# The low parts of split weights: VectorE takes the subtractions that Pool took in turn

## The chip, the core and the metric

The kernel runs on one core of a Trainium2 chip. The metric is the device time of one execution in microseconds (us). The engines are TensorE (PE, matrix products; its weight loads are listed as PEld), VectorE (DVE), ScalarE (ACT), GpSimd (Pool) and SyncE (SP), whose queue issues most DMAs. Each engine works through its own instructions in order and waits for the others by semaphores.

## The reference

Two blocks of network follow each other on 256 tokens of width 1024, everything in float32:

```python
def first_block(x, ...):                       # two layers
    for l in range(DEPTH):
        mix = even_mixer(...) if l % 2 == 0 else odd_mixer(...)
        x = layer_norm(ALPHA * x + mix, ln_g[l, 0], ln_b[l, 0])
        ffn = routed_moe(x, router_w, router_b, moe_w_gate[l], moe_w_up[l], moe_w_down[l])
        x = layer_norm(ALPHA * x + ffn, ln_g[l, 1], ln_b[l, 1])

def second_block(x, c, ada_w, ada_b, ...):     # two layers of three sublayers
    mod = c_act @ ada_w[layer] + ada_b[layer]  # shift, scale, gate of each sublayer
    x = x + 0.5 * (1 + gate) * swiglu(modulate(x, 0), ...)
    x = x + (1 + gate) * (hybrid_mixer | mlstm_block)(modulate(x, 1), ...)
    x = x + 0.5 * (1 + gate) * swiglu(modulate(x, 2), ...)

def swiglu(h, w_gate, w_up, w_down):
    return (jax.nn.silu(h @ w_gate) * (h @ w_up)) @ w_down
```

What matters here is that every weight is used once, for 256 tokens, and that most products are wanted more exact than one pass of PE gives.

## The kernel before, in words

The program is ten phases, one after the other, named by letters: A the even attention mixer, B its experts, C the odd attention mixer, D its experts, and then in the second block E, G, H and J, the four SwiGLU feed-forward sublayers, with F (the hybrid of a linear recurrence and a state-space layer) between E and G, and I (the mLSTM) between H and J.

The weights of all phases come from memory in one long sequence of 1 MB DMAs (128 partitions of 2048 floats, `load_weights`, L507), issued from SP. Each holds two chunks of 128x1024. The chunks land in blocks of a common pool of 23 blocks of 8 KB per partition; a block is given back when the work on it is done, and the next DMA of the sequence waits for a free block. A dry run beforehand fixes at which points of the program DMAs are issued.

A chunk of the ordinary weights is split before use (`new_split`, L579): ACT copies it rounded to the 32-bit format that PE takes in one pass (the high part, L586), and a second engine subtracts that copy from the chunk to give the low part (L587). A product is then three passes on PE (L594): high by high, low by high, high by low. PE's passes on a chunk can begin with the high part, but not end without the low one. The two expert phases B and D use their weights unsplit, so L587 doesn't appear there.

Which engine subtracts is what the change is about. In the kernel before, `pool=True` sends a subtraction to Pool; besides, a counter `nsplit` sends every third one there, every fourth in C, G and H, every sixth in F (`POOL_SPLIT`). Two places pause that: after the gate weights of the mLSTM are prepared `no_pool` counts 14 splits, and after each recurrence of F six. All others go to DVE.

`pool=True` is given at two places: `following` (L967) makes the first splits of the next phase while the last one ends, and does so with Pool for phases C and E (three and three); `enter` (L891) makes one more at the start of E.

Other work on the same queues, which the numbers below name:
- L545, in `ada_step`: the modulation of the second block (`mod`) is a product of one vector with a very long weight matrix. Its chunks come in the same sequence of DMAs, and DVE multiplies each by the vector and adds up, in one instruction over 128x1024 floats. These stand between the splits, at points that the plan fixes.
- L646 and L647: the high part (ACT) and the low part (DVE) of an activation, 128x256.
- L1858 and L1999: convolution and state products of F on DVE, with small tiles.
- L2088 to L2103, `gate_weights`: in the middle of phase H, 864 KB of gate columns for phase I are loaded, Pool clears a buffer (L2091), and builds the gate weights by small multiplications and additions (L2099, L2102, L2103). The block that the columns lay in is free after the last of them.
- L800 to L815 and L853 to L897: the layer norm at the end of a layer of the first block and the norm behind it, one token block of 128 after the other.

The order within each engine is set by a scheduler that takes the program's order as base and lets some instructions go earlier by a priority (`sooner`, with `SPLIT_AHEAD` for splits and `ADA_AHEAD` for L545), according to the costs it assumes for each engine.

Of the kernel before, what the change touches and what calls it, by code (L numbers as in the profile page):

```python
# [322 lines left out]
class Pipe:  # L323


    def __init__(self, sooner):
        self.waiting, self.flying, self.sooner = [], [], sooner
# [40 lines left out]

SLACK = {'A': 5, 'B': 3, 'C': 7, 'D': 2, 'E': 6, 'F': 7, 'G': 7, 'H': 7, 'I': 6, 'J': 7}

POOL_SPLIT = {'C': 4, 'F': 6, 'G': 4, 'H': 4}
POOL_TURN = {}
POOL_P = ''

PIECES = ((slice(0, 512), slice(512, 1024)),) * 2
# [18 lines left out]
class Net:  # L394
    NBLK = 23

    def __init__(self, ctx, tc, aps, phases, plan=None, at=None):
        self.tc, self.nc, self.aps, self.phases = tc, tc.nc, aps, phases
        self.blk = ctx.enter_context(tc.tile_pool(name="blk", bufs=1))
        self.cst = ctx.enter_context(tc.tile_pool(name="cst", bufs=1))  # L400
        self.sm = ctx.enter_context(tc.tile_pool(name="sm", bufs=2))
        self.pp = ctx.enter_context(tc.tile_pool(name="pp", bufs=4, space=bass.MemoryType.PSUM))
        self.issue_at, self.at = plan, at or {}
        self.free = [(-64, 0, b) for b in range(self.NBLK if plan is not None else 64)]
        self.own, self.nfree = {}, 0
        self.uid = 0
        self.nchunk = sum(NCH[p] for p in phases)
        self.ndma = (self.nchunk + 1) // 2
        self.issued = 0
        self.ring = {}  # L410
        self.pos = 0
        self.nsplit, self.phase, self.last_mm, self.last_pe = 0, None, [], None
        self.held, self.no_pool = [], 0
        self.hold, self.closed, self.span = False, [], {}
        self.pre, self.guard, self.guarded, self.evac = [], [], 0, None
        self.first, self.last, self.left = {}, {}, {}
# [162 lines left out]
    def new_split(self, n, pool=False):  # L579
        i, w = self.raw()  # L580
        u, t = self.alloc([128, 2, 1024], F32R)
        self.nsplit += 1
        self.no_pool -= 1
        eng = self.nc.gpsimd if pool or self.no_pool < 0 and (self.nsplit + POOL_TURN.get(self.phase, 0)) % POOL_SPLIT.get(self.phase, 3) == 0 else self.nc.vector
        with self.sooner(SPLIT_AHEAD.get(self.phase, 0)):
            self.nc.scalar.activation(t[:, 0, :n], w[:, :n], AF.Copy)  # L586
            eng.tensor_tensor(t[:, 1, :n], w[:, :n], t[:, 0, :n].bitcast(F32), op=OP.subtract)  # L587
        self.taken(i)
        return u, t[:, 0, :n], t[:, 1, :n]
# [1218 lines left out]
    def phase_ffn(self, l, s, nxt):  # L1808
        nc = self.nc
        us, xt, room = self.entry  # L1810
        token = self.first4(xt, room)
        acc = self.acc4()
        nt = 6
        items, hl = [], []
        ur, ring = self.alloc([128, 4, 2, S], F32R)
        for f in range(24):
            if f == 22 - nt:
                uk = [self.alloc([128, 4, 2, S], F32R) for _ in range(nt // 3)]
            if f < 22:
                if f < 4:  # L1820
                    u = self.p1(xt, ps=self.ph)
                    g = token(f)
                else:
                    g = self.p1(xt, ps=self.ph)
                    u = self.p1(xt, ps=self.ph)
                a = self.w0()
                i = f - 22 + nt
                p = uk[i // 4][1][:, i % 4] if i >= 0 else ring[:, f % 4]
                nc.scalar.activation(a, g, AF.Silu)  # L1829
                nc.vector.tensor_tensor(a, a, u, op=OP.mult)  # L1830
                self.hilo(a, p[:, 0, :], p[:, 1, :])
                hl.append((p[:, 0, :], p[:, 1, :]))
                if f == 6 and nxt == (1, 1):
                    self.gate_weights()
                    self.no_pool = 14
                if f == 21:
                    self.warm(AF.Sqrt, a)
                    self.prep_gate(l, s)
                    if nxt:
                        self.prep(*nxt)  # L1840
            if f >= 24 - nt:
                items.append((hl[f - 2], self.split()))
            elif f >= 2:
                self.row(acc, hl[f - 2], f == 2, False)
            if f == 23 - nt:
                self.release(ur)
        self.release(*us)
        self.tail(acc, items, self.gated(l, s, self.following()))
        self.release(*(u for u, _ in uk))
# [11 lines left out]
    def phase_F(self):  # L1861
# [26 lines left out]
        def gates(h):  # L1888
            rec[h] = self.alloc([128, 2, 4, S])
            for j in range(4):  # L1890
                n = 4 * h + j
                for a, bname in enumerate(('lba', 'lbx')):
                    ps = self.ph()
                    self.mm(ps[:, :S], ws[a][:, n, :], xl[:, n, :])
                    nc.scalar.activation(rec[h][1][:, a, j, :], ps[:, :S], AF.Sigmoid, bias=self.col(bname, n))

        def recur(h):
            u, ri = rec[h]
            r, gi, tt = ri[:, 0], ri[:, 1], tts[:, h]
            for j in range(4):  # L1900
                n = 4 * h + j
                nc.scalar.activation(tt[:, j, :], r[:, j, :], AF.Tanh, scale=lam[:, 1, n:n + 1])
                nc.scalar.activation(r[:, j, :], r[:, j, :], AF.Exp, scale=lam[:, 0, n:n + 1])
                a2 = self.w0()
                nc.gpsimd.tensor_tensor(a2, r[:, j, :], r[:, j, :], op=OP.mult)
                v.scalar_tensor_tensor(tt[:, j, :], a2, 1.0, tt[:, j, :], op0=OP.add, op1=OP.mult)
                nc.gpsimd.tensor_tensor(gi[:, j, :], gi[:, j, :], xl[:, n, :], op=OP.mult)
            nc.scalar.activation(flat(tt), flat(tt), AF.Sqrt)
            for j in range(4):
                n = 4 * h + j  # L1910
                nc.gpsimd.tensor_tensor(tt[:, j, :], tt[:, j, :], gi[:, j, :], op=OP.mult)  # L1911
                v.tensor_tensor_scan(xl[:, n, :], r[:, j, :], tt[:, j, :], 0.0, op0=OP.mult, op1=OP.add)
            self.release(u, lag=1)

        for i in range(8):
            self.conv(token(i) if i < 4 else self.p1(xt), 'lcw', 'lcb', i, xl[:, i, :])
            if i == 3:
                wa = self.raw()
                self.ada_step()
                wx = self.raw()  # L1920
                self.ada_step()
                ws = [a[1].rearrange("p (n o) -> p n o", n=8) for a in (wa, wx)]
            if i == G0:
                gates(0)
            if i == R0:
                recur(0)
                self.no_pool = 6
        uz, zz = self.alloc([128, 8, S])
        for i in range(8):
            v.tensor_copy(zz[:, i, :], self.p1(xt))  # L1930
            if i == G1:
                gates(1)
                self.done(wa[0])
                self.done(wx[0])
            if i == R1:
                recur(1)
                self.no_pool = 6
        self.release(utt, lag=2)
        uhi, yhi = self.alloc([128, 8, S], F32R)
        ulo, ylo = self.alloc([128, 8, S], F32R)  # L1940
# [454 lines left out]
```

## Time and profile before

| | |
|---|---|
| median of 3 runs | 1922.91 us (1920.03 to 1923.42) |
| profiled execution | 1923.58 us, of which the span from first to last instruction 1921.9 |
| PE busy | 1842.1 us (96%) |
| DVE busy | 1196.6 us (62%) |
| ACT busy | 879.4 us (46%) |
| Pool busy | 460.7 us (24%) |
| mean granted clock of TensorE | 0.986 of full speed |
| subtractions L587 | 297 on DVE, 117 on Pool |

The busy times are sums over stages with different limits. In the rows further down, a timeline row gives the start (us from the begin of the span), the duration, the engine, the line and operation, the tile written and those read, and in brackets how long the engine had stood idle and what it had waited for. "t" is any block of the pool, "pg" and "ph" are PSUM tiles, "kc" a constant.

### The profile page before, as it was taken

The numbers are of one execution on the slowest core, as the hardware profiler recorded it, in microseconds if no ns is written. First come the engines' busy times: TensorE is split into PE (matmuls) and PEld (weight loads), VectorE is DVE, ScalarE is ACT, GpSimd is POOL, SyncE is SP. The second block draws the span as 40 slices with busy tenths as digits, with TensorE's granted clock in tenths as the row PEclk, the third lists the DMA queues.
The fourth block names the chain that finished last, engine by engine and source line by source line (L and its number), as shares of the span: only waits on it lengthen the run. The fifth ranks groups of instructions, "written<-read, shape, count | busy, mean of one in ns | idle before, by whom it ended". The sixth has DMA issues, their size and how long they took to land.

```text
span 1921.9 us, 29062 instructions
## 1 busy us (share of the span) xinstructions
PE 1842.1 (96%) x11556; PEld 1477.0 (77%) x11556; DVE 1196.6 (62%) x1948; ACT 879.4 (46%) x1523; POOL 460.7 (24%) x295
## 2 busy tenths in 40 slices
PE   7999999889999998999999999999999999999998
PEld 7874544577544547999898779998899888879997
DVE  5862221586422229899699987767797665576453
ACT  5641111355221125445686644455345566655443
POOL 2200000231000004334243222222423213443232
PEclk9999999989999998999999999999999999999999
DMA  9569999565899996883435478647674615555520
GB/s 386 225 239 389 422 420 421 235 234 209 332 420 421 420 421 269 349 339 150 163 132 219 165 295 324 268 178 295 254 322 176 258 72 181 212 208 211 198 88 34
DMA packets 70975, 507.01 MB, mean 264 GB/s; under 512 B 7856, under 2 KB 8112, under 8 KB 10032
## 3 DMA queue, kind: packets, MB, share of 16 engines
q1 hardware_dynamic: 70256, 503.15, 65.9%
q8 instruction: 92, 1.51, 0.3%
q10 hardware_dynamic: 576, 1.93, 0.3%
q14 instruction: 51, 0.42, 0.1%
HBM read 504.00 MB, written 1.05 MB: 263 GB/s over the span
## 4 chain that ended last, share of the span: by engine, by line
PE 45%; DVE 10%; POOL 4%; ACT 3%; issue 3%; DMA 2%; DVEq 0%; POOLq 0%; ACTq 0%
PE ph L594 27%; PE pg L594 16%; DVE t L587 3%; DMA t<-in_weights 2%; DVE t L1858 2%; PE ph L599 1%; DVE t L545 1%; POOL t L587 1%; ACT t L586 1%; POOL w L2266 1%; POOL t L1911 0%; POOL t L2103 0%; DVE t L1999 0%; ACT ph L851 0%; ACT t L1855 0%
## 5 line engine op out<-in xcount | busy, mean ns | idle before, releaser
L594 PE MATMUL pg<-t,t 128*128 128x512 f32 (+4 forms) x4702 | 941.1, 403 | 27.4 <-DVE t L587 9.9
L594 PEld LDWEIGHTS pg<-t,t 128*128 128x128 f32 (+1 forms) x4702 | 674.7, 180 | 236.8 <-issue 126.0
L594 PE MATMUL ph<-t,t 128*128 128x256 f32 (+3 forms) x4550 | 589.5, 290 | 7.5 <-ACT t L2130 2.3
L594 PEld LDWEIGHTS ph<-t,t 128*128 128x128 f32 (+2 forms) x4550 | 564.5, 192 | 23.5 <-issue 3.1
L586 ACT ACTIVATE t<-t 128x1024 fp32r<-128x1024 f32 (+4 forms) x414 | 425.0, 1049 | 255.9 <-DVE t L587 73.0
L587 POOL TENSOR_TENSOR t<-t,t 128x1024 fp32r<-128x1024 f32 (+2 forms) x117 | 303.8, 2601 | 882.7 <-ACT t L586 778.4
L587 DVE TENSOR_TENSOR t<-t,t 128x1024 fp32r<-128x1024 f32 (+1 forms) x297 | 414.8, 1412 | 107.1 <-ACT t L586 105.6
L545 DVE SCALAR_TENSOR_TENSOR t<-t,cact 128x1024 f32<-128x1024 f32 x144 | 222.7, 1558 | 34.6 <-DMA t<-in_weights 30.8
L594 PE MATMUL ph<-t,w 128*64 128x512 f32 (+3 forms) x696 | 161.5, 547 | 0.0
L594 PEld LDWEIGHTS ph<-t,w 128*64 128x64 f32 (+1 forms) x696 | 68.4, 145 | 73.7 <-issue 63.5
L1353 DVE TENSOR_TENSOR w<-w,pg 128x512 f32<-128x512 f32 x16 | 10.9, 684 | 154.7 <-ACT w L1352 154.7
L1352 ACT ACTIVATE w<-pg 128x512 f32<-128x512 f32 x16 | 9.6, 598 | 186.4 <-PE pg L594 186.4
L646 ACT ACTIVATE t<-w 128x256 fp32r<-128x256 f32 x107 | 43.8, 411 | 107.1 <-DVE w L1830 94.8
L1381 DVE SCALAR_TENSOR_TENSOR t<-ph,rgsl,t 128x512 fp32r<-128x512 f32 x32 | 24.0, 751 | 108.4 <-ACT t L1380 108.4
L647 DVE TENSOR_TENSOR t<-w,t 128x256 fp32r<-128x256 f32 x96 | 75.4, 785 | 21.6 <-ACT t L646 21.5
L1380 ACT ACTIVATE t<-ph,rgsl 128x512 fp32r<-128x512 f32 x32 | 22.0, 687 | 128.3 <-PE ph L594 128.3
L1830 DVE TENSOR_TENSOR w<-w,ph 128x256 f32<-128x256 f32 x88 | 36.6, 416 | 50.8 <-PE ph L594 50.2
L599 PE MATMUL ph<-kc,t 128*128 128x128 f32 x248 | 40.5, 291 | 23.0 <-DVE t L897 10.5
L599 PEld LDWEIGHTS ph<-kc,t 128*128 128x128 f32 x248 | 29.3, 147 | 31.3 <-issue 12.2
L1829 ACT ACTIVATE w<-ph 128x256 f32<-128x256 f32 x88 | 32.7, 372 | 42.1 <-PE ph L594 34.8
L1626 POOL MEMSET t<- 64x256 f32 x2 | 0.6, 307 | 212.8 <-DMA t<-in_weights 211.8
L594 PE MATMUL ph<-w,t 128*128 128x256 f32 (+2 forms) x384 | 51.1, 306 | 0.2 <-DVE t L1304 0.2
(335 smaller groups left out, 1389.5 us busy)
## 6 DMA issues: line engine op xcount, KB each, us to landing
t<-in_weights SPq DMA_DIRECT2D x475, 1024.0 KB, 8.6
t<-in_xT SPq DMA_DIRECT2D x2, 512.0 KB, 5.4
t<-in_weights SPq DMA_DIRECT2D x2, 512.0 KB, 6.3
t<-in_x SPq DMA_DIRECT2D x1, 1024.0 KB, 12.6
t<-in_gate_cols ACTq DMA_DIRECT2D x1, 864.0 KB, 8.2
t<-in_consts_attn SPq DMA_DIRECT2D x1, 512.0 KB, 18.6
t<-in_final_g ACTq DMA_DIRECT2D x1, 512.0 KB, 3.7
out<-t SPq DMA_DIRECT2D x2, 256.0 KB, 2.0
```

The source lines that it names most:

```text
L545: self.nc.vector.scalar_tensor_tensor(w, w, 1.0, self.cact, op0=OP.mult, op1=OP.mult, accum_out=acc)
L586: self.nc.scalar.activation(t[:, 0, :n], w[:, :n], AF.Copy)
L587: eng.tensor_tensor(t[:, 1, :n], w[:, :n], t[:, 0, :n].bitcast(F32), op=OP.subtract)
L594: self.last_mm = [self.nc.tensor.matmul(out, lhsT=a, rhs=b, start=start, stop=stop)]
L599: self.last_pe = self.nc.tensor.transpose(out, a, self.ident)
L646: self.nc.scalar.activation(hi, src, AF.Copy)
L647: (eng or self.nc.vector).tensor_tensor(lo, src, hi.bitcast(F32), op=OP.subtract)
L1380: self.evac = nc.scalar.activation(yy[:, 0, ns], y[n], AF.Copy, scale=gsl[:, pr % 2, :])
L1381: v.scalar_tensor_tensor(yy[:, 1, ns], y[n], gsl[:, pr % 2, :], yy[:, 0, ns].bitcast(F32), op0=OP.mult, op1=OP.subtract)
L1829: nc.scalar.activation(a, g, AF.Silu)
L1830: nc.vector.tensor_tensor(a, a, u, op=OP.mult)
L1858: nc.vector.scalar_tensor_tensor(dst[:, sh:], ps[:, :S - sh], self.col(w + str(j), i), dst[:, sh:], op0=OP.mult, op1=OP.add)
```

## The change

The tables `POOL_SPLIT` and `POOL_TURN`, the counter and both pauses go. A subtraction is Pool's only where `pool=True` is given; that leaves seven, three for C and four for E. 110 go to DVE. Lines move up by two to seven: L587 becomes L583, L586 L582, L545 L543, L2091 L2084.

```diff
--- before.py
+++ after.py
@@ -368,8 +368,6 @@
 
 SLACK = {'A': 5, 'B': 3, 'C': 7, 'D': 2, 'E': 6, 'F': 7, 'G': 7, 'H': 7, 'I': 6, 'J': 7}
 
-POOL_SPLIT = {'C': 4, 'F': 6, 'G': 4, 'H': 4}
-POOL_TURN = {}
 POOL_P = ''
 
 PIECES = ((slice(0, 512), slice(512, 1024)),) * 2
@@ -409,8 +407,8 @@
         self.issued = 0
         self.ring = {}
         self.pos = 0
-        self.nsplit, self.phase, self.last_mm, self.last_pe = 0, None, [], None
-        self.held, self.no_pool = [], 0
+        self.phase, self.last_mm, self.last_pe = None, [], None
+        self.held = []
         self.hold, self.closed, self.span = False, [], {}
         self.pre, self.guard, self.guarded, self.evac = [], [], 0, None
         self.first, self.last, self.left = {}, {}, {}
@@ -579,9 +577,7 @@
     def new_split(self, n, pool=False):
         i, w = self.raw()
         u, t = self.alloc([128, 2, 1024], F32R)
-        self.nsplit += 1
-        self.no_pool -= 1
-        eng = self.nc.gpsimd if pool or self.no_pool < 0 and (self.nsplit + POOL_TURN.get(self.phase, 0)) % POOL_SPLIT.get(self.phase, 3) == 0 else self.nc.vector
+        eng = self.nc.gpsimd if pool else self.nc.vector
         with self.sooner(SPLIT_AHEAD.get(self.phase, 0)):
             self.nc.scalar.activation(t[:, 0, :n], w[:, :n], AF.Copy)
             eng.tensor_tensor(t[:, 1, :n], w[:, :n], t[:, 0, :n].bitcast(F32), op=OP.subtract)
@@ -1832,7 +1828,6 @@
                 hl.append((p[:, 0, :], p[:, 1, :]))
                 if f == 6 and nxt == (1, 1):
                     self.gate_weights()
-                    self.no_pool = 14
                 if f == 21:
                     self.warm(AF.Sqrt, a)
                     self.prep_gate(l, s)
@@ -1924,7 +1919,6 @@
                 gates(0)
             if i == R0:
                 recur(0)
-                self.no_pool = 6
         uz, zz = self.alloc([128, 8, S])
         for i in range(8):
             v.tensor_copy(zz[:, i, :], self.p1(xt))
@@ -1934,7 +1928,6 @@
                 self.done(wx[0])
             if i == R1:
                 recur(1)
-                self.no_pool = 6
         self.release(utt, lag=2)
         uhi, yhi = self.alloc([128, 8, S], F32R)
         ulo, ylo = self.alloc([128, 8, S], F32R)
```

The engines' order follows. The first place is DVE at the end of phase D and the start of phase E, where the layer norm of the first token block (L800 to L815) and the norm behind it (L853 to L897) are worked off. Before:

```order
L800 BN_AGGR lnmv_5587<-lnst_5586 128x2
L810 SCALAR_TENSOR_TENSOR t_67<-pg_5524,lnmv_5587,t_5356 128x512
L812 RECIPROCAL lnrs_5588<-lnrs_5588 128x1
L810 SCALAR_TENSOR_TENSOR t_67<-pg_5526,lnmv_5587,t_5356 128x512
L815 SCALAR_TENSOR_TENSOR t_67<-t_67,lnrs_5588,t_5356 128x512 x2
L795 BN_STATS lnst_5586<-pg_5530 128x6
L853 TENSOR_TENSOR rms_5650<-ss_5649 128x1
L857 RECIPROCAL rms_5650<-rms_5650 128x1
L897 TENSOR_SCALAR t_5585<-t_67,rms_5650 128x512 x2
```

and now, where the rows on t_5455, t_5463 and t_5465 are products of the modulation:

```order
L796 BN_AGGR lnmv_5587<-lnst_5586 128x2
L543 SCALAR_TENSOR_TENSOR t_5455,mod<-t_5455,cact 128x1024
L806 SCALAR_TENSOR_TENSOR t_67<-pg_5524,lnmv_5587,t_5356 128x512
L808 RECIPROCAL lnrs_5588<-lnrs_5588 128x1
L806 SCALAR_TENSOR_TENSOR t_67<-pg_5526,lnmv_5587,t_5356 128x512
L811 SCALAR_TENSOR_TENSOR t_67<-t_67,lnrs_5588,t_5356 128x512 x2
L791 BN_STATS lnst_5586<-pg_5530 128x6
L543 SCALAR_TENSOR_TENSOR t_5463,mod<-t_5463,cact 128x1024
L849 TENSOR_TENSOR rms_5650<-ss_5649 128x1
L853 RECIPROCAL rms_5650<-rms_5650 128x1
L543 SCALAR_TENSOR_TENSOR t_5465,mod<-t_5465,cact 128x1024
L893 TENSOR_SCALAR t_5585<-t_67,rms_5650 128x512 x2
```

Three modulation products now stand inside the chain; before, all came after it.

The second place is Pool in phase H, ahead of the gate weights of the mLSTM. Before:

```order
L587 TENSOR_TENSOR t_11638<-t_11525,t_11638 128x1024
L587 TENSOR_TENSOR t_11774<-t_11533,t_11774 128x1024
L587 TENSOR_TENSOR t_11874<-t_11539,t_11874 128x1024
L587 TENSOR_TENSOR t_11986<-t_11641,t_11986 128x1024
L2091 MEMSET t_12022 128x1024
L2102 TENSOR_TENSOR t_12022<-t_12020 128x128
L2099 TENSOR_TENSOR t_12022<-t_12020 128x16x8 x2
```

and now:

```order
L666 TENSOR_TENSOR t_11352<-w_1811_11434,t_11351 128x2x128
L666 TENSOR_TENSOR t_11352<-w_1823_11512,t_11351 128x2x128
L2084 MEMSET t_12022 128x1024
L2095 TENSOR_TENSOR t_12022<-t_12020 128x128
L2092 TENSOR_TENSOR t_12022<-t_12020 128x16x8 x2
```

The four subtractions are gone; the clearing of the buffer (t_12022) follows the low parts of the sublayer's input (L666).

The third place is DVE at the start of H. Before:

```order
L545 SCALAR_TENSOR_TENSOR t_11527,mod<-t_11527,cact 128x1024
L587 TENSOR_TENSOR t_11602<-t_11525,t_11602 128x1024
L587 TENSOR_TENSOR t_11677<-t_11527,t_11677 128x1024
L920 COPY t_11353<-pg_11567 128x512
L587 TENSOR_TENSOR t_11716<-t_11529,t_11716 128x1024
```

and now:

```order
L543 SCALAR_TENSOR_TENSOR t_11527,mod<-t_11527,cact 128x1024
L583 TENSOR_TENSOR t_11602<-t_11525,t_11602 128x1024
L583 TENSOR_TENSOR t_11638<-t_11525,t_11638 128x1024
L916 COPY t_11353<-pg_11567 128x512
L583 TENSOR_TENSOR t_11677<-t_11527,t_11677 128x1024
```

The subtraction for t_11638, the first of Pool's four above, is now the second in DVE's queue, and the one for t_11677 moves behind the copy.

## Rows read from the trace of the kernel before

**Rows 1.** The page: busy time of each engine.
```profile
PE 1842.1 (96%) x11556; PEld 1477.0 (77%) x11556; DVE 1196.6 (62%) x1948; ACT 879.4 (46%) x1523; POOL 460.7 (24%) x295
```

**Rows 2.** Windows, all engines; the first line names the columns.
```profile
core 0: us, PE busy (x) PEld busy (x) DVE busy (x) ACT busy (x) POOL busy (x), PEclk, DMA share, GB/s
...
768.00:912.00 144.00, 144.00 (x1041) 136.67 (x1041) 128.80 (x146) 69.71 (x95) 53.02 (x19) 1.00 0.70 279
1008.00:1056.00 48.00, 45.50 (x372) 42.69 (x371) 47.55 (x91) 33.24 (x60) 17.46 (x15) 1.00 0.60 224
...
1390.00:1395.00 5.00, 5.00 (x16) 4.17 (x16) 5.00 (x7) 4.13 (x7) 0.00 (x0) 0.50 1.00 424
```

**Rows 3.** Lines by shape: count, busy us, mean ns, idle before and releaser.
```profile
L587 DVE TENSOR_TENSOR t<-t,t 128x1024 fp32r<-128x1024 f32 x291 | 406.2, 1411 | 103.8 <-ACT t L586 102.3 <-issue 0.8
L587 POOL TENSOR_TENSOR t<-t,t 128x1024 fp32r<-128x1024 f32 x110 | 290.6, 2645 | 873.7 <-ACT t L586 777.9 <-issue 27.7 <-DMA t<-in_weights 26.4
...
L545 DVE SCALAR_TENSOR_TENSOR t<-t,cact 128x1024 f32<-128x1024 f32 x144 | 222.7, 1558 | 34.6 <-DMA t<-in_weights 30.8 <-ACT cact L755 3.7
```

**Rows 4.** Line L587 alone: min, median, max in ns.
```profile
L587 DVE TENSOR_TENSOR t<-t,t x297: 949/1220/3441, 7.2 to 1881.1; 128x1024 fp32r<-128x1024 f32 x146, 128x972 fp32r<-128x972 f32 x2, 128x968 fp32r<-128x968 f32 x1
```

**Rows 5.** Timeline in F: start, us, engine, line, tiles, idle before.
```profile
1049.30 2.39 POOL L587 TENSOR_TENSOR t<-t,t 128x1024 fp32r<-128x1024 f32 x1 [3.85 <-ACT t L586]
1049.37 2.61 DVE L1999 SCALAR_TENSOR_TENSOR t<-t,dts,t 128x256 f32<-128x256 f32 x1
...
1052.63 0.47 DVE L1999 SCALAR_TENSOR_TENSOR t<-t,dts,t 128x256 f32<-128x256 f32 x1
```

**Rows 6.** Timeline, end of D and start of E.
```profile
716.84 7.47 POOL L587 TENSOR_TENSOR t<-t,t 128x1024 fp32r<-128x1024 f32 x3 [222.63 <-ACT t L586]
...
727.00 1.94 PE L599 MATMUL ph<-kc,t 128*128 128x128 f32 x8 [4.16 <-DVE t L897]
...
741.52 3.42 DVE L545 SCALAR_TENSOR_TENSOR t<-t,cact 128x1024 f32<-128x1024 f32 x1
...
750.06 0.45 PE L599 MATMUL ph<-kc,t 128*128 128x128 f32 x1 [2.98 <-DVE t L920]
```

**Rows 7.** Timeline in H, around the gate weights.
```profile
1348.41 0.38 ACTq L2088 DMA_DIRECT2D t<-in_gate_cols  x1
...
1359.22 2.75 POOL L587 TENSOR_TENSOR t<-t,t 128x1024 fp32r<-128x1024 f32 x1 [12.28 <-ACT t L586]
...
1362.84 0.52 POOL L2102 TENSOR_TENSOR t<-t 128x128 f32<-128x128 f32 x1
...
1389.18 4.64 PE L594 MATMUL pg<-t,t 128*128 128x512 f32 x10 [3.76 <-DVE t L587]
```

**Rows 8.** The page: DMA of the gate columns, us to landing last.
```profile
t<-in_gate_cols ACTq DMA_DIRECT2D x1, 864.0 KB, 8.2
```

**Rows 9.** The chain of waits in H: start, us, what.
```profile
1381.10 5.56 DMA t<-in_weights
```

**Rows 10.** Timeline, start of H.
```profile
1323.73 2.43 POOL L587 TENSOR_TENSOR t<-t,t 128x1024 fp32r<-128x1024 f32 x1 [3.03 <-PE pg L594]
...
1323.84 4.53 DVE L587 TENSOR_TENSOR t<-t,t 128x1024 fp32r<-128x1024 f32 x2
...
1327.30 2.90 PE L594 MATMUL ph<-t,t 128*128 128x256 f32 x22 [2.02 <-DVE t L587]
```

**Rows 11.** Windows, line L587 alone: length, DVE busy (x), POOL busy (x).
```profile
0.00:144.00 144.00, 25.77 (x18) 22.43 (x9) 1.00 0.72 284
336.00:500.00 164.00, 20.32 (x14) 19.90 (x8) 0.95 0.60 238
960.00:1104.00 144.00, 55.47 (x39) 15.54 (x6) 0.99 0.47 170
```

**Rows 12.** Timeline, start of G.
```profile
1143.20 2.12 PE L594 MATMUL pg<-t,t 128*128 128x512 f32 x8 [1.08 <-DVE t L647]
```

**Rows 13.** Windows, a stretch of I, columns as in rows 2.
```profile
1637.00:1712.00 75.00, 72.40 (x429) 61.75 (x428) 47.97 (x62) 48.26 (x71) 38.94 (x28) 1.00 0.54 211
```

## What was predicted

> **What bounds the kernel now.** I read the busy line first. TensorE (PE) is busy 1842.1 of 1921.9 us, VectorE (DVE) 1196.6, Pool 460.7 [rows 1]. So nearly everything that a change elsewhere can win or lose lies in the roughly 80 us in which PE does nothing, plus the stretches in which it runs at half clock; a mean of 62% on DVE says little by itself. Next I cut the span into stages. In the steady part of phase E PE has no idle time at all (144.00 of 144) although DVE is busy 128.80 and Pool's 19 instructions fill 53.02 [rows 2]: a faster DVE is worth nothing there, and a slower one has 15 us to spare. In the middle of phase F it is the other way round: DVE is busy 47.55 of 48 us and PE 45.50 [rows 2].
>
> The third view groups instructions by line and shape. A low-part subtraction of a 128x1024 chunk takes 1411 ns on DVE and 2645 ns on Pool; an adaptive product (L545) takes 1558 ns on DVE [rows 3]. The single line shows more: the subtraction on DVE has a median of 1220 ns, but a longest of 3441 [rows 4]. The fourth view, the timeline, shows where the long ones lie. At 1049.30 Pool begins a subtraction of 2.39 us, and the small DVE product that begins at 1049.37 takes 2.61 us; the same line takes 0.47 at 1052.63, with no subtraction on Pool [rows 5]. An adaptive product beside Pool's subtraction takes 3.42 [rows 6]. So a DVE instruction with two SBUF inputs that meets a Pool subtraction stands still for about 2.1 us (2.61 − 0.47). [...]
>
> **The change, part by part.** It takes the turn counter and its two pauses away. 110 subtractions go from Pool to DVE; Pool keeps seven named ones, three at the start of C and four at the start of E. ACT's copies, PE's products and the DMAs are the same in number.
>
> *DVE's total.* Added: 110 × 1.22 = 134 us [rows 4]. Given back: what L587 and L545 now take beyond 1.22 us each, 406.2 − 291 × 1.22 = 51 and 222.7 − 144 × 1.22 = 47 [rows 3, 4], 98 together, and something more from the smaller products (the 0.47 that became 2.61). Between 98 and the full 134 given back, DVE's busy time comes to 1197 (the 1196.6 of now) to 1233 us. So on the whole DVE pays for its new work with the stalls that go, and time moves only where a stall, or Pool's own 2.6 us, sits in front of PE. These places follow.
>
> *Gate weights in H (L2088 to L2103).* The 864 KB of gate columns are issued at 1348.41 [rows 7] and take 8.2 us [rows 8], so they are there at about 1356.6. But Pool's queue holds four subtractions ahead of the MEMSET, as the order shows, the last from 1359.22 for 2.75 us, and the first product begins at 1362.84 [rows 7]. The products end at 1381.1, a block comes free, a weight DMA of 5.56 us starts [rows 9], and PE stands still for 3.76 us at 1389.18 for a subtraction on that weight [rows 7], after which it runs at a granted clock of 0.50 from 1390 to 1395 [rows 2]. Without the four subtractions the chain can begin at 1356.6, 6.2 us earlier. That is more than the gap of 3.76, so the gap goes, and with it most of the half clock (5 us at 0.50 are 2.5 us lost; part of it would be lost to the next hole). Bounds: 0 (another weight of that batch is late in its place) and −6.3 (3.76 + 2.5). I take −5.5, since the order shows nothing else ahead of the MEMSET.
>
> *Start of H.* PE waits 2.02 us at 1327.30 for two DVE subtractions that take 4.53 us beside Pool's at 1323.73 [rows 10]. After the change the three stand one behind the other on DVE (the order: t_11602, t_11638): the first pair takes 2 × 1.22 = 2.44. Bounds 0 and −2.1; I take −2.
>
> *F.* Six Pool subtractions lie between 960 and 1104 beside 39 on DVE [rows 11]. On a full DVE each costs 2.1 of stall and now 1.22 of work, so −0.9 each, −5.3 in all if DVE sets the pace everywhere, and +7.3 (6 × 1.22) if no stall goes. PE's own 2.5 us of idle in 48 [rows 2] says that only part of DVE's time shows; I take −4.
>
> *G, I, A, C.* At 1143.20 PE waits 1.08 us for an L647 product that took 2.51 [rows 12]: −1. In I PE is idle for 2.6 of the 75 us from 1637 to 1712, while Pool works 38.94 [rows 13], some of it on subtractions that PE's weights wait for: −2, between 0 and −2.6. In A nine go from Pool [rows 11]; by the F price of 0.9 that is −8 if all of DVE's time showed; the entry waits for transfers as well, so I take −1. In C five of eight go and the three named ones stay; the top-k chain keeps DVE, so 0, between −4.5 (5 × 0.9) and +6.1 (5 × 1.22).
>
> *End of D, start of E: a loss.* The four named subtractions stay on Pool (716.84, 7.47 us for three) and PE waits 4.16 us at 727.00 for the normalised token block [rows 6]. The order now places adaptive products inside that layer-norm chain: one ahead of L806, two more before L893. Three cost 3 × 1.22 = 3.7 us on the path, and up to 3 × 3.42 = 10.3 [rows 6] if each meets Pool; none if DVE would have waited in the same place anyhow. Behind them fewer are left, and Pool's next subtractions are gone, so the wait of 2.98 us at 750.06 [rows 6], which stood behind a stalled product, should give back some 1.7. Together +2.
>
> *Rest of E, G, H and all of J.* Nothing: PE covers it, as in 768 to 912 [rows 2]. The cover is 15 us of DVE in that stretch; if it is gone, see the second rival.
>
> Sum: −5.5 − 2 − 4 − 1 − 2 − 1 + 0 + 2 = −13.5. The profiled execution took 1923.58 (span 1921.9 and 1.7 around it): 1910.1. The median of the runs lies 0.7 below the profiled one, so 1909.
>
> **The rivals.**
> *No change (1919 to 1927).* Each removed wait is replaced by the next one: in H another weight of the same batch, in F the ACT copies, in I the recurrence. For it: PE is 96% busy [rows 1], and five of my terms are 2 us or less. Against: the H chain has a named cause with 6 us of slack behind it.
> *Slower (1942).* DVE becomes the bound. This holds if the stalls are not given back, because Pool's remaining work of other kinds takes their place beside the new, denser DVE queue. Then every moved subtraction costs 1.22: in 768 to 912 DVE needs 128.80 + 19 × 1.22 = 152 us for 144, so +8 [rows 2]; F +7.3; the start of E +3.7: +19, or 1942. It decides from the point where DVE's mean for a 128x1024 subtraction stays at 1.41 or above with 407 of them. For it: the full DVE in F. Against: the stalls in the timeline lie beside Pool's subtractions. [...]
> *Twice as much (1893).* All of the idle PE time behind DVE goes: −6.3 in H, −2.1, −5.3 in F, −8 in A, −4.5 in C, −2.6 in I, −1 in G, 0 at E: −30. For it: a PE that waits less keeps its clock. Against: in A and C transfers and the top-k bound the chain.
> *Only H (1916).* The change doesn't remove the contention where it hurts most, since the seven named subtractions still stand beside the two layer-norm chains, and the smaller terms cancel: −5.5 − 2.
>
> **How the numbers follow.** Forecast 0.50, only H 0.13, twice as much 0.10, no change 0.14, slower 0.13. A measurement of this kernel can tell about 0.2%, 3.9 us, from no change. Faster: 0.50 + 0.13 + 0.10 = 0.73; within: 0.14; slower: 0.13. The range leaves out the slower rival and half of the biggest gains: 1894 to 1927. The likeliest case's own range is 1903 to 1916.
>
> **What would show it.** Right: 407 subtractions on DVE with a mean of 1.22 to 1.30; adaptive products near 1.25; DVE busy 1197 to 1233; Pool's MEMSET of the gate weights at its data's landing and no PE gap of 3.8 us there; PE's busy time unchanged. E's start is right if its PE gap grows beyond 4.16. Wrong: DVE's mean still near 1.41, or new PE waits for L583 in phase E or J, or the H gap still there behind another weight.

## Result: 1888.6 us, 1.8% faster, below the predicted range

The changed kernel takes 1888.63 us (median of 4 runs, 1888.08 to 1889.17), the kernel before 1923.16 beside it: a ratio of 0.9824, 95% interval 0.9811 to 0.9836. The prediction was 1909 with a range down to 1894. The direction and the main cause were right, the size was not: 34.5 us instead of 14.

The page of the changed kernel, busy time of each engine, answers to [rows 1]:

```profile
PE 1831.7 (97%) x11556; PEld 1469.1 (78%) x11556; DVE 1172.7 (62%) x2058; ACT 882.2 (47%) x1523; POOL 185.4 (10%) x185
```

DVE has 110 more subtractions and is busy 23.9 us less. 110 × 1.22 = 134 us of work came, so some 158 us of stalls went. The span is 1887.3. The gain shows on PE in two parts: it stands idle 55.6 us instead of 79.8 (span less busy), and the same 11556 products take 10.4 us less. The mean granted clock is 0.992 instead of 0.986, by estimate some 12 us less lost to a lower clock (0.014 × 1921.9 against 0.008 × 1887.3); a new order of PE's products in F takes 4.4 us of it back (below).

The lines by shape, answering to [rows 3] (count, busy us, mean ns), and windows, answering to [rows 2] and, in the last, [rows 13] (length, then PE, PEld, DVE, ACT, POOL busy, PEclk, DMA share, GB/s):

```profile
L583 DVE TENSOR_TENSOR t<-t,t 128x1024 fp32r<-128x1024 f32 x397 | 483.9, 1238 | 118.5 <-ACT t L582 117.0 <-PE pg L590 0.8
...
L543 DVE SCALAR_TENSOR_TENSOR t<-t,cact 128x1024 f32<-128x1024 f32 x144 | 179.3, 1254 | 24.6 <-DMA t<-in_weights 24.5
```

```profile
750.20:894.20 144.00, 144.00 (x1041) 136.67 (x1040) 114.48 (x159) 71.51 (x96) 0.00 (x0) 1.00 0.74 294
989.00:1036.00 47.00, 45.84 (x369) 42.67 (x368) 45.30 (x90) 32.62 (x59) 8.25 (x10) 1.00 0.64 243
...
1369.40:1374.40 5.00, 5.00 (x31) 5.00 (x31) 4.51 (x7) 2.39 (x4) 0.00 (x0) 0.66 0.86 342
1607.00:1682.00 75.00, 75.00 (x444) 64.57 (x442) 52.75 (x71) 48.73 (x72) 23.96 (x21) 1.00 0.57 227
```

Both means fell to 1.24 and 1.25 us. In E the stretch of 144 us, in which Pool subtracted 19 times, needs less of DVE than before (114 against 129 us). In F DVE is still nearly full (45.30 of 47). In H a stretch at less than full clock is left (0.66 over 5 us, before 0.50), and in I PE has no idle time where it had 2.6 us.

Where the time came from is read by laying PE's n-th instruction of one trace beside the n-th of the other. PE has 11556 in both, so the difference of their starts is the time won up to there, and its change over a phase is what that phase gave. In us, from the profiled executions (minus is earlier; the runs of the other columns follow below):

| | predicted | changed kernel | before_noread | ghost_read | late_low |
|---|---|---|---|---|---|
| A | −1 | −8.6 | −7.2 | −4.0 | −7.3 |
| C | 0 | −11.7 | −4.6 | −7.6 | −10.9 |
| D | | +0.9 | 0.0 | +0.9 | +0.9 |
| E | +2 | +1.6 | −3.6 | +11.0 | +1.7 |
| F | −4 | +1.8 | −4.2 | +14.6 | +3.3 |
| G | −1 | −4.2 | −4.1 | −1.5 | −3.4 |
| H | −7.5 | −4.7 | −9.3 | +0.4 | −4.2 |
| I | −2 | −9.9 | −10.8 | −5.4 | −7.0 |
| J | 0 | +0.2 | +0.2 | +0.3 | 0.0 |
| sum | −13.5 | −34.6 | −43.6 | +8.7 | −26.9 |

A, C and I gave 30 of the 35 us; I had put 3 there.

### The profile page after: what moved, and what is told of

Read it like the earlier page. It is cut to its first block, busy times and chain, and to the rows that moved or that the text cites. A ratio compares the mean times of both kernels' runs of the same rounds, so it can differ in the third digit from the quotient of the medians.

```text
span 1887.3 us, 28933 instructions
## 1 busy us (share of the span) xinstructions
PE 1831.7 (97%) x11556; PEld 1469.1 (78%) x11556; DVE 1172.7 (62%) x2058; ACT 882.2 (47%) x1523; POOL 185.4 (10%) x185
## 4 chain that ended last, share of the span: by engine, by line
PE 56%; DVE 4%; DMA 3%; ACT 2%; issue 1%; POOL 1%; DVEq 0%; POOLq 0%; ACTq 0%; SPq 0%
PE ph L590 31%; PE pg L590 24%; DMA t<-in_weights 3%; PE ph L595 1%; DVE t L583 1%; DVE t L543 1%; ACT t L582 1%; POOL t L1906 0%; DVE t L893 0%; DVE t L941 0%; DVE w L939 0%; ACT ph L847 0%; DVE t L643 0%; POOL w L1900 0%; ACT t L1850 0%
## 5 line engine op out<-in xcount | busy, mean ns | idle before, releaser
L583 DVE TENSOR_TENSOR t<-t,t 128x1024 fp32r<-128x1024 f32 (+2 forms) x407 | 493.3, 1231 | 122.0 <-ACT t L582 120.4
L582 ACT ACTIVATE t<-t 128x1024 fp32r<-128x1024 f32 (+4 forms) x414 | 426.1, 1051 | 235.2 <-PE ph L590 78.8
L543 DVE SCALAR_TENSOR_TENSOR t<-t,cact 128x1024 f32<-128x1024 f32 x144 | 179.3, 1254 | 24.6 <-DMA t<-in_weights 24.5
L1349 DVE TENSOR_TENSOR w<-w,pg 128x512 f32<-128x512 f32 x16 | 10.9, 684 | 154.7 <-ACT w L1348 154.7
L941 POOL TENSOR_TENSOR t<-t,w 128x512 f32<-128x512 f32 x12 | 15.6, 1303 | 666.7 <-DVE w L939 666.7
L642 ACT ACTIVATE t<-w 128x256 fp32r<-128x256 f32 x107 | 43.6, 409 | 54.4 <-DVE w L1826 47.5
L595 PE MATMUL ph<-kc,t 128*128 128x128 f32 x248 | 38.9, 284 | 19.5 <-DVE t L893 13.5
L847 ACT ACTIVATE ph<-t 128x512 f32<-128x512 f32 x28 | 16.9, 602 | 76.9 <-POOL t L941 41.1
L590 PEld LDWEIGHTS ph<-w,t 128*128 128x128 f32 (+1 forms) x384 | 40.3, 172 | 14.0 <-issue 8.6
L643 DVE TENSOR_TENSOR t<-w,t 128x256 fp32r<-128x256 f32 x96 | 44.5, 464 | 8.7 <-ACT t L642 8.7
```

The source lines that it names most:

```text
L543: self.nc.vector.scalar_tensor_tensor(w, w, 1.0, self.cact, op0=OP.mult, op1=OP.mult, accum_out=acc)
L590: self.last_mm = [self.nc.tensor.matmul(out, lhsT=a, rhs=b, start=start, stop=stop)]
L595: self.last_pe = self.nc.tensor.transpose(out, a, self.ident)
L642: self.nc.scalar.activation(hi, src, AF.Copy)
L643: (eng or self.nc.vector).tensor_tensor(lo, src, hi.bitcast(F32), op=OP.subtract)
L847: nc.scalar.activation(junk[:, :ns.stop - ns.start], xs, AF.Square, accum_out=ss[:, n:n + 1])
```

## Experiments

Three theories were set against each other. S: the gain is stalls of DVE beside Pool's reading. L: it is that Pool hands over a low part later than DVE does. O: it is the order that the scheduler makes of the changed program.

**ghost_read and ghost_write: Pool at work, but not needed.** Both are the changed kernel with something added at the 110 old places, where `ghost` is true (its line is left out here).

```diff
+            if ghost:                      # ghost_read, behind DVE's subtraction
+                h = t[:, 0, :n].bitcast(F32)
+                self.nc.gpsimd.tensor_tensor(w[:, :n], h, h, op=OP.subtract)

+            if ghost:                      # ghost_write, ahead of DVE's subtraction
+                self.nc.gpsimd.memset(t[:, 1, :n].bitcast(F32), 0.0)
```

> The changed kernel, and at the 110 places where Pool subtracted before, Pool once more runs a subtraction of the same size behind ACT's copy; its result goes into the used-up chunk and nobody reads it. DVE does all the subtractions as in the changed kernel, and PE's order is the changed kernel's. Theory S (the gain is stalls of DVE beside Pool's reading): the stalls come back and the 134 us of added DVE work stay, so L587's mean on DVE is 1.4 or above, the modulation products are at 1.5, and the time goes to 1915 to 1945. Rival L (the gain is that a low part comes from DVE after 1.22 us and not from Pool after 2.6): the low parts still come from DVE, so 1889 to 1897. Rival O (the gain is the scheduler's new order of the queues): the order is kept, so 1889 to 1893.

> The changed kernel, and at the same 110 places Pool clears the low part's buffer before DVE's subtraction overwrites it: Pool is at work but reads nothing. Theory S in the form that Pool's reading stalls DVE: 1889 within 3, and L587's mean on DVE stays at 1.23. If any work of Pool stalls DVE: 110 x 0.95 us of clearing beside it, up to 104 us of stalls on DVE, L587's mean at 1.35 or above and 1900 or more. Rivals L and O: 1889 to 1892.

ghost_read took 1932.82 us (1932.25 to 1935.91), slower than the kernel before: ratio 1.0063 (1.0044 to 1.0081). ghost_write took 1890.17 (1888.76 to 1892.86), ratio 0.9837 (0.9818 to 0.9856). The lines by shape, of ghost_read first:

```profile
L588 DVE TENSOR_TENSOR t<-t,t 128x1024 fp32r<-128x1024 f32 x397 | 557.6, 1424 | 99.3 <-ACT t L587 97.5 <-PE pg L598 0.8
L591 POOL TENSOR_TENSOR t<-t 128x1024 f32<-128x1024 f32 x106 | 249.8, 2360 | 672.2 <-DVE t L588 477.2 <-issue 119.5 <-DMA t<-in_weights 27.3
L545 DVE SCALAR_TENSOR_TENSOR t<-t,cact 128x1024 f32<-128x1024 f32 x144 | 201.1, 1405 | 21.1 <-DMA t<-in_weights 21.1
```

```profile
L591 DVE TENSOR_TENSOR t<-t,t 128x1024 fp32r<-128x1024 f32 x397 | 484.5, 1239 | 117.3 <-ACT t L588 112.2 <-POOL t L590 1.8 <-ACT t L650 1.2
L590 POOL MEMSET t<- 128x1024 f32 x106 | 101.2, 958 | 750.2 <-PE ph L598 286.6 <-PE pg L598 216.8 <-DVE t L591 143.2
```

A reading Pool whose results nobody wants costs 44 us and puts DVE's mean back to 1424 ns; a writing Pool costs nothing that can be told (1239 ns). PE's order is the changed kernel's in ghost_read, and in ghost_write but for six rows. S holds. The 44 us are not the reading alone: the ghost also keeps its chunk and the high part occupied until it is done (ACT's copies wait 74 us for it in all, 52 for Pool in the kernel before); before_noread, below, takes away the reading by itself. The modulation products missed my number (1.405, not 1.5): a ghost reads one tile twice and starts later than Pool's subtraction did, so it doesn't copy the old stalls exactly.

**before_noread: only the stalls taken away.** The kernel before, in its order (but for some 20 of PE's rows), with Pool occupied and the low part late for nearly as long (by the means 0.40 + 0.96 + 0.96 = 2.31 us a place, where a subtraction of Pool took 2.65), but without reading chunks. The low parts at these 110 places are left out.

```diff
-            eng.tensor_tensor(t[:, 1, :n], w[:, :n], t[:, 0, :n].bitcast(F32), op=OP.subtract)
+            if eng is self.nc.gpsimd and not pool and self.issue_at is not None:
+                eng.tensor_copy(t[:, 1, :1], t[:, 0, n - 1:n].bitcast(F32))
+                eng.memset(t[:, 1, :n].bitcast(F32), 0.0)
+                eng.memset(t[:, 1, :n].bitcast(F32), 0.0)
+            else:
+                eng.tensor_tensor(t[:, 1, :n], w[:, :n], t[:, 0, :n].bitcast(F32), op=OP.subtract)
```

> The kernel before with its turns, but at Pool's 110 unnamed places Pool, behind ACT's copy, copies one column and clears the low part's buffer twice (0.5 + 2 x 0.95 = 2.4 us) in place of subtracting: those low parts are left out (zero), Pool is as long at work and the low part as late as before, and nothing of Pool reads a chunk. DVE keeps its 297 subtractions and, but for some 20 rows, its order. Theory S: the stalls go at once, L587's mean on DVE is 1.23 to 1.25, DVE's busy time 1196.6 - 158 = 1040, and the time falls to 1885 to 1900 (what remains is Pool's latency, 8 us in the run with late low parts). Rival O: the order is before's, so most of the gain stays away, 1910 to 1922. Mixed: if phase C comes only 4 us earlier and not 11.7, its remaining 7 were the order.

It took 1878.86 us (1876.24 to 1880.03), ratio 0.9767 (0.9746 to 0.9788): 44 us less, more than the change itself brought and more than S had said. The page's engines and two lines by shape:

```profile
PE 1829.8 (97%) x11556; PEld 1470.1 (78%) x11556; DVE 1053.7 (56%) x1948; ACT 882.6 (47%) x1523; POOL 420.5 (22%) x515
...
L592 DVE TENSOR_TENSOR t<-t,t 128x1024 fp32r<-128x1024 f32 x291 | 357.0, 1239 | 138.2 <-ACT t L586 137.1 <-issue 0.4
L545 DVE SCALAR_TENSOR_TENSOR t<-t,cact 128x1024 f32<-128x1024 f32 x144 | 177.2, 1241 | 34.1 <-DMA t<-in_weights 33.8
```

The stalls were 142.9 us of DVE's time (1196.6 − 1053.7) and 44 us of the kernel's. So taking the stalls away alone gives 44; the change gives 34.5. (The left-out low parts are zeros in PE's products. Whether that matters was not tested; the mean granted clock is 0.992 as in the changed kernel.) The table says where the change falls short: E and F (two orders, below) and H. In C the stalls are worth 4.6 and not 11.7: there O has a share, and ghost_read, with the new order and a reading Pool, keeps 7.6 of C's gain. The timeline of C shows one place, before_noread first, then the changed kernel:

```profile
398.56 1.06 ACT L586 ACTIVATE t<-t 128x1024 fp32r<-128x1024 f32 x1 [3.17 <-POOL t L1725]
399.64 1.20 ACT L1735 ACTIVATE t<-pg 64x256 f32<-64x256 f32 x4
...
400.07 2.93 PE L599 MATMUL pg<-t,t 128*128 128x512 f32 x6 [3.59 <-ACT t L1735]
```

```profile
395.56 0.93 ACT L1726 ACTIVATE t<-pg 64x256 f32<-64x256 f32 x3
...
395.99 1.66 PE L590 MATMUL pg<-t,t 128*128 128x512 f32 x6 [0.18 <-ACT t L1726]
...
399.30 1.06 ACT L582 ACTIVATE t<-t 128x1024 fp32r<-128x1024 f32 x1 [0.64 <-POOL t L1716]
```

In the old order ACT's high-part copy, which waits for Pool, stands ahead of the evacuation that PE waits for; in the new order the evacuation (L1726) stands first, and PE waits 0.18 us instead of 3.59, about half of the 7 us.

**late_low: the low part late, without reading.** The changed kernel, with Pool writing into the low part's buffer ahead of DVE's subtraction (clears of 0.96 and 0.53 us, behind a copy of one column of 0.50).

```diff
+            if ghost:
+                lo = t[:, 1, :n].bitcast(F32)
+                self.nc.gpsimd.tensor_copy(t[:, 1, :1], t[:, 0, n - 1:n].bitcast(F32))
+                self.nc.gpsimd.memset(lo, 0.0)
+                self.nc.gpsimd.memset(lo[:, :n // 2], 0.0)
```

> The changed kernel; at the 110 places Pool, as soon as ACT's copy is there, copies one column into the low part's buffer and clears it one and a half times (about 1.5 us without reading a chunk), and DVE's subtraction overwrites it afterwards. So the low part is as late as Pool's was (1.5 + 1.2 = 2.7 us behind ACT), but nothing of Pool reads beside DVE. Theory S: no stalls, so the time stays at 1889 to 1893, and L587's mean at 1.24. Rival L: what the ghost subtractions left of the gain (A 4.1, C 7.5, I 5.3 us) goes here, so 1900 to 1908.

1897.08 us (1894.63 to 1897.66), ratio 0.9861 (0.9845 to 0.9878): between the two forecasts. Pool's latency is worth some 8 us against the changed kernel, 2.9 of it in I and 1.3 in A by the table (C 0.8). The 7.6 us that ghost_read had kept in C are not this latency: late_low keeps 10.9 of 11.7 there. The kernel's order of PE differs in some 60 rows from the changed kernel's, so the 8 us are a rough figure.

**change_ACI and change_EFGHJ: half of the change each.**

```diff
-        eng = self.nc.gpsimd if pool or self.no_pool < 0 and ...
+        eng = self.nc.gpsimd if pool or self.phase not in 'ACI' and self.no_pool < 0 and ...
```

(an edit of the kernel before, with 'EFGHJ' in the other run.)

> The change in phases A, C and I alone; E, F, G, H and J give Pool its turns as before. By the shift of PE's instructions between the two traces (A 8.6, C 11.7, I 9.9 us earlier): 1923.2 - 30.2 = 1893. By the terms of the prediction (A 1, C 0, I 2): 1920.

> The change in phases E, F, G, H and J alone; A, C and I give Pool its turns as before. By the shift between the two traces (E 1.6 later, F and the start of G 2.4 earlier, H 4.7 earlier): 1923.2 - 5.5 = 1918. By the terms of the prediction (E +2, F 4, G 1, H 7.5): 1913.

change_ACI took 1904.76 (1902.91 to 1909.23), ratio 0.9908 (0.9890 to 0.9926); change_EFGHJ 1910.29 (1907.00 to 1912.31), ratio 0.9941 (0.9919 to 0.9962). Both missed. In change_ACI the changed phases came out as in the whole change (A −8.6, C −11.4, I −10.2), but phases that were not changed moved too: E lost 6.3 us and F 6.7. (Its profiled execution, 1909.23 us, was the slowest of its four, so these losses may be larger than usual.) In change_EFGHJ G gave 4.1 us as in the whole change, but H gave 7.2 instead of 4.7, E gave 4.7 where the whole change loses 1.6, and I, not changed, gave 3.4. PE's wait at the start of E, in change_ACI:

```profile
713.03 1.94 PE L599 MATMUL ph<-kc,t 128*128 128x128 f32 x8 [9.30 <-DVE t L897]
```

The order of that kernel has the three modulation products inside the layer-norm chain; that of change_EFGHJ has them behind it. So the loss at E is brought by the change in the phases ahead of it, through the scheduler. The 6.7 us that F lost in change_ACI lie at one place, where a weight comes late:

```profile
887.65 3.28 POOL L587 TENSOR_TENSOR t<-t,t 128x1024 fp32r<-128x1024 f32 x1
888.60 2.62 DVE L647 TENSOR_TENSOR t<-w,t 128x256 fp32r<-128x256 f32 x1
...
902.15 1.06 ACT L586 ACTIVATE t<-t 128x1024 fp32r<-128x1024 f32 x1 [6.56 <-DMA t<-in_weights]
...
904.05 8.15 PE L594 MATMUL pg<-t,t 128*128 128x512 f32 x23 [3.83 <-ACT t L646]
```

The chain of waits leads from PE's gap of 3.83 us over ACT's copy to that weight's DMA, and from the DMA's start back over the stalled L647 (2.62 us beside Pool's subtraction). Behind the gap PE takes 0.35 us a product (23 in 8.15), where ten in the changed kernel at 1363.04 take 0.26 each (2.57). Why the same turns of Pool do no such harm there in the kernel before is not shown.

**walled and named_walled: the order at E mended, and Pool rid of the last seven.** walled lets the products of E be placed only behind the norm of the second token block; named_walled also puts the seven named subtractions on DVE.

```diff
+            if (l, s) == (0, 0):
+                self.wall = (i,)          # the last L893; self.wall = () at first
...
-            with self.sooner(ADA_AHEAD.get(self.phase, 0)):
+            with self.behind(*self.wall):
...
-        eng = self.nc.gpsimd if pool else self.nc.vector
+        eng = self.nc.vector              # named_walled alone
```

> The changed kernel with one order mended: the modulation products of phase E may only be placed behind the second token block's norm (L893). In the run in which C is unchanged PE's instructions at the start of E come 4.7 us earlier, with C changed 1.6 to 6.3 later; the order shows three products inside the layer-norm chain only with C changed. If they are the cause: PE's gap of 9.3 us at the start of E falls to 4 to 5 and the time to 1882 to 1885. If the four named subtractions on Pool are the cause: the gap stays above 7 and the time at 1887 to 1889.

> The changed kernel, the products walled off as in the run named walled, and the seven named subtractions on DVE as well, so Pool does none. Theory S: the stalls beside them in the two layer-norm chains go (in E 7.99 us of Pool's reading beside the chain, in C two PE gaps of 2.3 and 2.1); they cost 3 x 1.22 on DVE ahead of each chain, so about 2 us each are won: 1878 to 1883. If DVE's queue is what the chains wait for: 3.7 us lost at each, 1886 to 1892.

walled took 1883.38 (1882.18 to 1884.37), ratio 0.9794 (0.9778 to 0.9811); named_walled 1879.80 (1879.31 to 1886.67), ratio 0.9785 (0.9764 to 0.9806). PE's wait at the start of E, in the changed kernel with what stood in the chain, then in walled, then in named_walled:

```profile
697.40 7.99 POOL L583 TENSOR_TENSOR t<-t,t 128x1024 fp32r<-128x1024 f32 x3 [223.85 <-ACT t L582]
...
700.12 3.06 DVE L543 SCALAR_TENSOR_TENSOR t<-t,cact 128x1024 f32<-128x1024 f32 x1 [1.43 <-DMA t<-in_weights]
...
707.13 1.20 DVE L543 SCALAR_TENSOR_TENSOR t<-t,cact 128x1024 f32<-128x1024 f32 x1
...
708.87 1.22 DVE L543 SCALAR_TENSOR_TENSOR t<-t,cact 128x1024 f32<-128x1024 f32 x1
...
712.72 0.66 PE L595 MATMUL ph<-kc,t 128*128 128x128 f32 x2 [9.31 <-DVE t L893]
```

```profile
707.11 1.30 PE L595 MATMUL ph<-kc,t 128*128 128x128 f32 x5 [4.15 <-DVE t L893]
```

```profile
704.58 1.73 PE L595 MATMUL ph<-kc,t 128*128 128x128 f32 x7 [2.96 <-DVE t L893]
```

The wait fell from 9.31 to 4.15 us with the products out of the way, and to 2.96 without Pool's four. Both came out as expected; named_walled's second run has 2.95 us again. Run again beside the changed kernel on one chip:

> The changed kernel once more, beside the next one on the same chip: 1889.

> The run named_walled once more beside the changed kernel on the same chip: 1880, 9 us or 0.45% below it.

The changed kernel took 1888.48 (1888.12 to 1889.47), named_walled 1883.53 (1879.06 to 1886.88), 5 us below it and not 9; its ratio to the kernel before is 0.9792 (0.9766 to 0.9818) against 0.9821 (0.9802 to 0.9840). It is 5 to 9 us below the changed kernel, and its runs spread more; these intervals overlap. Whether the seven named ones add to walled's gain the times don't show (1883.38 against 1879.80 and 1883.53).

**allbutF: F left as it was.** An edit of the kernel before.

```diff
+        eng = ... pool or self.phase not in 'ACEGHIJ' and self.no_pool < 0 and ...
```

> The changed kernel, but phase F gives Pool every sixth subtraction as before (with its pauses). Theory S by the prediction's price (2.1 of stall against 1.22 of work): F gets worse by up to 5 us, 1889 to 1894. Rival: DVE is the bound in F and each subtraction moved there costs it 1.22: F gets better by up to 7 us, 1882 to 1887.

1888.84 us (1886.63 to 1892.72), ratio 0.9828 (0.9811 to 0.9844): the same as the changed kernel, between the two forecasts. In F the change is worth nothing either way. That is two things that cancel: F's stalls go, and PE's products come in a worse order, as the next part shows.

## Why the prediction was wrong, step by step

**The failed step is "time moves only where a stall, or Pool's own 2.6 us, sits in front of PE. These places follow".** The list was wrong: I had listed places with a long PE gap and taken A, I and G for small (−1, −2, −1). They gave 8.6, 9.9 and 4.2, and the stalls alone are worth 7.2, 10.8 and 4.1 there (before_noread). In A I had put −1 against an upper bound of −8 because "the entry waits for transfers as well"; that wait is one of 7.2 us at the start, it stayed, and the others went. The rule was too narrow as well: in C and F time moved by a new order on ACT and on PE, which is neither a stall nor Pool's own 2.6 us. The stalls hit short instructions in chains, as these two show. The timeline of the kernel before, in A and in I:

```profile
40.67 2.47 POOL L587 TENSOR_TENSOR t<-t,t 128x1024 fp32r<-128x1024 f32 x1 [6.30 <-ACT t L586]
40.84 2.58 DVE L982 TENSOR_TENSOR w<-w,t 8x256 f32<-8x256 f32 x1
...
43.80 0.23 PE L594 MATMUL ph<-t,selb 128*128 128x128 bf16 x1 [1.89 <-DVE t L983]
...
1557.13 2.39 POOL L587 TENSOR_TENSOR t<-t,t 128x1024 fp32r<-128x1024 f32 x1 [7.90 <-ACT t L586]
1557.29 2.25 DVE L865 SCALAR_TENSOR_TENSOR mod<-mod,cols 128x8 f32<-128x8 f32 x1
...
1569.91 2.43 PE L594 MATMUL ph<-t,t 128*32 128x256 f32 x11 [2.30 <-ACT t L2130]
```

An instruction on 128x8 elements took 2.25 us; in the changed kernel it takes 0.16. The PE gap of 2.30 us behind it in I was followed by half clock, as a window of the kernel before shows:

```profile
1572.00:1576.00 4.00, 4.00 (x20) 4.00 (x20) 0.29 (x1) 0.00 (x0) 0.00 (x0) 0.50 0.00 0
```

In the changed kernel neither is there: from 1534 to 1548, around the same instruction at 1538.05, PE is busy 14.00 of 14 us at a granted clock of 1.00.

**"PE's busy time unchanged" was wrong.** It fell by 10.4 us, about a third of the gain, although F's new order adds 4.4. I had counted a return of the clock in H alone.

**DVE's total, 1197 to 1233, was too high.** I had bounded the returned time by the work added, 134; 158 came back. The two lines that I had counted gave 51 (L583 is now at 397 × 1.22) and 222.7 − 179.3 = 43 of it; the other 64, two fifths, lay in other lines, 31 of it on the products of L647 (128x256, a mean of 785 ns, now 464).

**C, 0 between −4.5 and +6.1, missed.** The stalls gave 4.6; that this is my outer bound is chance, since that was five subtractions at a price net of DVE's work. The rest, about 7, is the new order. I had read the order of three places and not this one.

**H's gate weights, −5.5, was half right.** PE's gap of 3.76 shrinks to 0.27, but "another weight of that batch is late in its place" came true too: by PE's starts this stretch gave 5.5 us and then lost 3.3. The timeline of the changed kernel, answering to [rows 7]:

```profile
1322.59 0.38 ACTq L2081 DMA_DIRECT2D t<-in_gate_cols  x1
...
1333.98 0.96 POOL L2084 MEMSET t<- 128x1024 f32 x1 [33.85 <-PE ph L590]
1334.89 1.51 POOL L2095 TENSOR_TENSOR t<-t 128x128 f32<-128x128 f32 x1
...
1355.85 0.46 POOL L2096 TENSOR_TENSOR t<-t 128x128 f32<-128x128 f32 x1
...
1363.04 2.57 PE L590 MATMUL pg<-t,t 128*128 128x512 f32 x10 [0.27 <-DVE t L583]
...
1368.07 1.21 PE L590 MATMUL ph<-t,t 128*128 128x256 f32 x8 [2.17 <-DVE t L583]
```

With the same 8.2 us the columns were there at 1330.8, but Pool's clearing began at 1333.98, behind a PE product by the profile: the build did not start at the landing of its data. It takes 21.4 us (1334.89 to 1356.31), before 18.8 (1362.84 to 1381.61): one of its products takes up to 1.5 us while DVE runs an instruction of 1.2, and 0.46 while DVE is idle, and DVE is denser now (16.92 us busy of 21.42, before 13.20 of 18.77). Against PE, which was 22.7 us ahead by then, it started 5 us earlier and ended 2.6 earlier. Nor was Pool's queue needed for the gap: in before_noread, where Pool writes nearly as long at the four places ahead of the build, no gap followed and the stretch gave 6.8 us. Its build took 17.1 us, from the first of these rows to the end of the last:

```profile
1332.02 0.79 POOL L2107 TENSOR_TENSOR t<-t 128x128 f32<-128x128 f32 x1
...
1348.66 0.45 POOL L2108 TENSOR_TENSOR t<-t 128x128 f32<-128x128 f32 x1
```

H's start, −2, came as forecast (−2.3 by PE's starts).

**F, −4, was wrong in sign (+1.8), through an order that I hadn't read.** With nothing but the stalls gone F gains 4.2 (before_noread). The change takes the stalls away too, but near the end of F the scheduler puts PE's products that use 64 columns of the array (128*64 in the rows) in pairs between the others, where they stood in groups of eight. The windows of this stretch and one such group, the kernel before first, then the changed kernel (windows: length, then PE, PEld, DVE, ACT, POOL busy, PEclk, DMA share, GB/s):

```profile
1046.95:1065.78 18.83, 16.93 (x127) 13.73 (x125) 18.61 (x38) 9.76 (x17) 5.53 (x5) 1.00 0.36 126
...
1058.33 0.88 PE L594 MATMUL ph<-t,w 128*64 128x256 f32 x8
```

```profile
1027.85:1049.76 21.91, 21.34 (x128) 14.86 (x126) 17.85 (x39) 9.97 (x17) 2.98 (x4) 1.00 0.50 197
...
1039.35 0.65 PE L590 MATMUL ph<-t,w 128*64 128x256 f32 x2
```

Eight products took 0.88 us in a row, two now take 0.65, and PE is busy 4.4 us longer on the same work at a granted clock of 1.00, with DVE busy less. The stretch lasts 3.1 us longer; in the runs that leave F's split of work as it was (before_noread, change_ACI, allbutF) it does not. So this is not the rival "slower": DVE, though nearly full, did not become the bound.

**E, +2, was right in size and place** (+1.6; gap 9.31), from the order's rows. That the size fits is partly luck: the chain lost 5.2 us where I had 3.7, and the stretch behind it won 3.5 where I had 1.7.

The rival "twice as much", at 1893 and a chance of 0.10, was nearest; it held the right kind of reason, stalls everywhere, against which I had argued with "transfers and the top-k bound the chain". That a PE that waits less keeps its clock came out here as 55.6 us of idle instead of 79.8 at a mean granted clock of 0.992 instead of 0.986. Its sum is near partly by luck: its terms miss both ways (F −5.3 against +1.8, I −2.6 against −9.9).

What stays open: what the moves of C's new order beside the one shown are worth, and why the weight in change_ACI comes late there and not in the kernel before.

## What to carry to other kernels

Pool's reading beside DVE was not paid for here by its own busy time but by the instructions of DVE that it stopped; count the stalled instructions on all lines, most of all the small ones in dependent chains (2.25 us instead of 0.16), and where the trace shows half clock behind a PE gap, price it (0.50 over 4 us behind the gap of 2.30 in I). The idle engine's free help was a loan: 110 subtractions that took Pool some 290 us cost the kernel 44 by their stalls, 142.9 us of DVE's time. And a change of engine is also a change of order everywhere behind it: read the order at every PE gap and of PE's own products, not only where the edit stands. In this case the order gave some 7 us in C and took some 5 in E and 4 in F.

## What the runs showed of the hardware that was not expected

- A Pool instruction that only writes (110 clears of 0.96 us) left DVE's mean at 1239 ns, one that reads (2.36 us) put it at 1424.
- Not every DVE instruction stopped beside Pool's reading, and one that stopped did not read two tiles in SBUF. In the kernel before a product of an SBUF and a PSUM tile (L1830) took 0.42 us beside Pool's, as is the median of its 88, while a multiplication of one small SBUF tile (L1008), with a median of 0.16, took 2.34. The rule of the prediction, two SBUF inputs, leaves out such instructions, which stand in A's chains:

```profile
51.92 3.28 POOL L587 TENSOR_TENSOR t<-t,t 128x1024 fp32r<-128x1024 f32 x1 [8.78 <-ACT t L586]
...
52.88 2.34 DVE L1008 TENSOR_SCALAR mx<-mx 128x2 f32<-128x2 f32 x1
...
1286.70 2.40 POOL L587 TENSOR_TENSOR t<-t,t 128x1024 fp32r<-128x1024 f32 x1 [2.73 <-ACT t L586]
...
1288.25 0.42 DVE L1830 TENSOR_TENSOR w<-w,ph 128x256 f32<-128x256 f32 x1 [2.85 <-PE ph L594]
```

- The stall did not grow with the stopped instruction: 128x8 elements waited as long (2.25 us instead of 0.16) as 128x1024 (3.42 instead of 1.22 to 1.25).
- Pool was slowed as well: its building of the gate weights took 2.6 us more in all (21.4 against 18.8) beside a denser DVE, a product up to 1.5 us beside a DVE instruction and 0.46 beside none.
- The same PE products cost more in F where those on 64 columns alternate with those on 128: 21.34 us instead of 16.93, at a granted clock of 1.00 both times.
